# Attention operand loads issued from POOL, and a one-column product moved from POOL to ACT, in a two-block transformer kernel

## The chip, the cores and the metric

The kernel runs on one core of a Trainium2 chip. The metric is device time in microseconds of one execution, median of several runs; lower is better. The engines named below are PE (matrix products), PEld (its weight loads), DVE, ACT and POOL (elementwise work) and SP, which in the kernel before does nothing but issue DMAs. Each engine runs its own list of instructions in order.

## The reference

Two transformer blocks follow one another on a sequence of 2048 rows of width 1024, in float32. The first block is a short convolution mixer and then a stick-breaking attention with 8 heads of 64; the second has a pooled mixer and an attention over the best keys that a small index network picks. Cut to the two attentions:

```python
def _stick_breaking_attention(q, k, v):          # first block
    for blk in range(n_blocks):                   # blocks of 128 queries
        z = einsum("bhqd,bhkd->bhqk", qb, kf[:, :, :kl]) * scale
        mask = arange(kl)[None, :] < q_pos[:, None]
        log_one_minus = where(mask, log_sigmoid(-z), 0.0)
        rev = cumsum(log_one_minus, axis=3, reverse=True)
        weights = exp(where(mask, z + rev, -inf))
        outs.append(einsum("bhqk,bhkd->bhqd", weights, vf[:, :, :kl]))

def dsa_attention(q, k, v, q_idx, k_idx, w_idx):  # second block, per block of 128 queries
    logits = einsum('bqhd,bsd->bqhs', qib, kf_idx) * IDX_DIM ** -0.5
    score = einsum('bqhs,bqh->bqs', relu(logits), wb) * N_IDX_HEADS ** -0.5
    _, sel = top_k(where(causal, score, -inf), 256)
    s = einsum('bqhgd,bqkhd->bqhgk', qg, k_sel) * HEAD_DIM ** -0.5
    o = einsum('bqhgk,bqkhd->bqhgd', softmax(where(valid, s, -inf)), v_sel)
```

## The kernel before

A float32 product is made of three PE passes over a rounded part and a rest of each operand (L119 to L121, `lin<-act,fixedr`). The program is a set of Python generators, one for each phase, which `build()` runs one after the other or merges two by two: `merge((a, wa), (b, wb))` takes steps from both in the proportion of their weights. Behind that, a scheduler fixes for every engine one static order of its instructions, before anything runs; an engine that reaches an instruction whose data or buffer isn't there waits, and everything behind it on that engine waits too.

The phases in order: a (convolution mixer), b (projections of the first attention), c (stick-breaking attention), d (its output projection and norms), e and e2 (projections of the second block), f (index scores, search, attention over chosen keys) and g (output projection). Halves of 1024 rows are overlapped: c(0) with b(1), c(1) with d(0), e(0), e2; f's first part with d(1), e(1), e2; and the rest of f with g.

All DMAs go through `dma()` (L75 to L77) and so stand in one order on SP: weights from DRAM (`fixed<-in_w_in_dram`), the split weights that are kept for the second half (`kept_w_in<-fixedr`) and read again (`fixedr<-kept_w_in`, `fixedr<-kept_w_out`), results on their way to DRAM (`qis<-xe`, `cata<-ff`), and the operands of both attentions.

- **Stick-breaking, phase_c.** For each pair of heads p and each chunk g of 512 queries (a group: 4 x 2 in each half, 16 in all) it loads `cq` (`crr<-qst`, two tiles of two DMAs, a ring of 3), `ck` (`crr<-kst`, a ring of 4) and `cv` (`crf<-vst`, a ring of 2). Then, for four blocks of queries, chunks of keys and the two heads a: z on PE (L535, L536), a sigmoid on ACT (L538), its complement on ACT (L545) or, on the diagonal, DVE (L543), a running product on DVE (L548), the weights as a product of shifted columns (L549), the last column by itself on POOL (L551), four transposes on PE (L555), a copy on ACT (L557), and the product with v on PE (L563). Column `left`, by which L551 scales, comes from the chunk of keys before.
- **Scores, f_score.** For each of 8 index heads a tile `fqi` (`ffr<-qis`, two DMAs, a ring of 2), products on PE (L871, L872), relu on ACT (L874), and a weighted sum on DVE (L881), begun on POOL (L876) and masked on POOL (L890).
- **Attention over chosen keys, f_block.** For each block of 128 queries and each p a tile `fq` (`ffr<-q2s`, two DMAs, a ring of 2), products on PE (L1147, L1148), a masked maximum on DVE (L1149), exp on ACT (L1161), transposes (L1170), copies (L1172), and v's product (L1178). At the end of a block POOL spreads the reciprocal of the sums (L1190), PE broadcasts it (L1194), DVE scales the result (L1196), and POOL copies one column as a marker (L1199).

POOL also adds sums of squares in the norms (L309), does small steps of rope and of the pool mixer (L719, L724, L757, L805, L808), and the last additions of phase g (L1269, L1270).

Of the kernel before, what the change touches and what calls it, by code (L numbers as in the profile page):

```python
# [19 lines left out]
P = 128  # L20
# [35 lines left out]
def merge(*gens):  # L56
    run(merged(*gens))
# [11 lines left out]
class Build:  # L69
# [4 lines left out]

    def dma(self, out, in_):  # L75
        f = lambda ap: ap.bitcast(F32) if ap.dtype == F32R else ap
        self.nc.sync.dma_start(f(out), f(in_))  # L77

# [401 lines left out]
    def load_dup(self, tag, bufs, src, a, sl):  # L480

        t = self.turn(tag, bufs)
        for d in range(2):
            self.dma(t[d * 64 : (d + 1) * 64], src[a * 64 : (a + 1) * 64, :, sl])
        return t

    def load_stack(self, tag, bufs, src, sl):

        t = self.turn(tag, bufs)
        for s in range(2):  # L490
            self.dma(t[s * 64 : (s + 1) * 64], src[:, s, sl].rearrange("(a p) n -> p a n", a=2))
        return t
# [13 lines left out]
    def phase_c(self, h):  # L506
# [3 lines left out]
        for p in range(4):  # L510
            for g in (2 * h, 2 * h + 1):
# [5 lines left out]
                for c in range(g, -1, -1):  # L517
                    cs = slice((c % 2) * CH, (c % 2 + 1) * CH)
                    kt[c] = self.load_stack("ck", 4, self.kst[p][c // 2], cs)
                    if c == g or c % 2:  # L520
                        n = HT // P if c % 2 else HT // P // 2
                        v = self.turn("cv", 2)
                        self.dma(v[:, :n], self.vst[p][c // 2][: n * P, :].rearrange("(b p) d -> p b d", p=P))
                    vt[c] = v[:, c % 2 * 4 : c % 2 * 4 + 4]
                o = self.psum("o")
                for i in range(4):
                    qs = slice(i * P, (i + 1) * P)
                    prev = [None, None]
                    for c in range(g, -1, -1):
# [3 lines left out]
                        for a in range(2):  # L533
# [16 lines left out]
                            if c < g:  # L550
                                nc.gpsimd.tensor_tensor(s[:, W - 1 : W], s[:, W - 1 : W], left, ALU.mult)  # L551
                            prev[a] = e
# [298 lines left out]
    def f_score(self, qbs):  # L851
# [6 lines left out]
        for hd in range(8):  # L858
            q = self.turn("fqi", 2)
            rows = self.qis[h][:, hd, :, gl : gl + n * P]  # L860
            for d in range(2):
                self.dma(q[d * 64 : (d + 1) * 64], rows)
            for k, qb in enumerate(qbs):
# [258 lines left out]
    def f_block(self, qb):  # L1122
# [9 lines left out]
        for p in range(4):  # L1132
            kv = p // 2
            q = self.turn("fq", 2)
            for d in range(2):
                self.dma(q[d * 64 : (d + 1) * 64], self.q2s[h][:, 2 * p : 2 * p + 2, :, qs])
            pe = []
# [140 lines left out]
    def build(self):  # L1278
# [9 lines left out]
        with (  # L1288
# [18 lines left out]
            de = self.chain(self.phase_d(0, xb), lambda: self.phase_e(0), lambda: self.phase_e2([0, 1], self.h2))  # L1307
            merge((self.ahead(self.phase_c(1), 2000), 260), (de, 300))
            self.f_setup(0)
# [134 lines left out]
```

## Time and profile before

| | us |
|---|---|
| median of 3 runs (3470.65 to 3471.43) | 3471.29 |
| the profiled execution | 3474.31 |
| its span (first to last instruction) | 3472.6 |
| PE busy | 3222.2 (93%) |
| DVE busy | 2256.2 (65%) |
| ACT busy | 1482.4 (43%) |
| POOL busy | 484.3 (14%) |

The mean granted clock of PE over the span was 0.962 of full speed. In a profile, a line such as L551 is one of the program above; out<-in are the program's tiles, with crf and crr the rings of the stick-breaking attention, ff and ffr those of phase f, and fixed, fixedr work buffers. A wait is put down to whatever ended last before the waiting instruction. Issuing a DMA isn't counted as busy; SPq is SP's queue of DMAs.

### The profile page before, as it was taken

Reading aid. Unit: us, or ns where it says so; the run is one execution under the profiler, and the core shown is the slowest. Engines: PE = TensorE matmul, PEld = TensorE weight load, DVE = VectorE, ACT = ScalarE, POOL = GpSimd, SP = SyncE. Lnnn points to the kernel's source line nnn. Section 1 sums busy time; section 2 is a strip of 40 time slices with the busy share of each in tenths; the row PEclk is TensorE's granted clock in tenths of the full one; section 3 lists DMA queues with packets and bytes.
Section 4 is the critical chain, followed back from the end, with each engine's and each line's share of the span. In section 5 each row is a group of like instructions: output and inputs, shape, how many; then the busy total and the mean of one; then the engine's idle time right before and its main releaser. Section 6 shows DMA issues by size and latency. Waiting matters only on the chain. (4 is left out here: it accounts for less than half of the span.)

```text
span 3472.6 us, 49120 instructions
## 1 busy us (share of the span) xinstructions
PE 3222.2 (93%) x17922; PEld 2569.6 (74%) x17922; DVE 2256.2 (65%) x4508; ACT 1482.4 (43%) x2668; POOL 484.3 (14%) x600
## 2 busy tenths in 40 slices
PE   8999999999999999988989998899898898889897
PEld 7888888888787777766767776677676676667675
DVE  5343544553535887788777787897447569888641
ACT  4111421111323444555545555563364365865561
POOL 0000110000100000142021112420200422102002
PEclk9999999999999999989999999899899999989999
DMA  3111442343464545645445444644433542115005
GB/s 108 49 47 52 157 160 83 127 131 107 143 173 140 173 130 153 200 152 139 145 152 178 131 133 137 191 149 145 153 104 107 164 158 95 47 43 174 25 29 174
DMA packets 369231, 438.66 MB, mean 126 GB/s; under 512 B 23504, under 2 KB 269776, under 8 KB 368976
## 3 DMA queue, kind: packets, MB, share of 16 engines
q1 hardware_dynamic: 368976, 435.38, 40.1%
q8 instruction: 145, 2.38, 0.3%
q14 instruction: 110, 0.90, 0.1%
HBM read 308.94 MB, written 124.78 MB: 125 GB/s over the span
## 5 line engine op out<-in xcount | busy, mean ns | idle before, releaser
L119 PE MATMUL lin<-act,fixedr 128*128 128x512 f32 x1488 | 603.6, 406 | 23.5 <-DMA fixedr<-kept_w_in 12.1
L120 PE MATMUL lin<-act,fixedr 128*128 128x512 f32 x1488 | 601.3, 404 | 12.8 <-DVE act L620 10.8
L121 PE MATMUL lin<-act,fixedr 128*128 128x512 f32 x1488 | 598.1, 402 | 0.0
L104 ACT ACTIVATE fixedr<-fixed 128x512 fp32r<-128x512 f32 x295 | 186.9, 634 | 730.0 <-PE lin L120 249.3
L548 DVE TENSOR_TENSOR_SCAN crf<-crf 128x512 f32<-128x512 f32 (+3 forms) x320 | 355.5, 1117 | 64.0 <-ACT crf L545 60.9
L119 PEld LDWEIGHTS lin<-act,fixedr 128*128 128x128 f32 x1488 | 286.8, 193 | 92.2 <-DMA fixedr<-kept_w_in 10.1
L120 PEld LDWEIGHTS lin<-act,fixedr 128*128 128x128 f32 x1488 | 286.0, 192 | 80.5 <-DVE act L620 14.9
L105 DVE TENSOR_TENSOR fixedr<-fixed,fixedr 128x512 fp32r<-128x512 f32 x295 | 204.3, 693 | 204.3 <-ACT fixedr L104 192.7
L121 PEld LDWEIGHTS lin<-act,fixedr 128*128 128x128 f32 x1488 | 285.8, 192 | 63.2
L1149 DVE CUSTOM_DVE_ANT_0 fe<-z,masks 128x512 f32<-128x512 f32 (+3 forms) x320 | 186.8, 606 | 151.7 <-PE z L1148 107.2
L557 ACT COPY crf<-tp 128x512 f32<-128x512 f32 (+3 forms) x320 | 164.5, 532 | 184.0 <-PE tp L555 166.9
L119 PE MATMUL z<-act,fixedr 128*128 128x512 f32 x584 | 231.1, 396 | 10.9 <-ACT fixedr L104 10.9
L538 ACT ACTIVATE crf<-z 128x512 f32<-128x512 f32 (+3 forms) x320 | 174.9, 548 | 136.3 <-PE tp L555 114.4
L121 PE MATMUL z<-act,fixedr 128*128 128x512 f32 x584 | 229.8, 394 | 0.0
L120 PE MATMUL z<-act,fixedr 128*128 128x512 f32 x584 | 229.7, 394 | 0.0
L1172 ACT COPY ff<-tp 128x512 f32<-128x512 f32 (+3 forms) x320 | 160.1, 522 | 156.6 <-PE tp L1170 89.4
L551 POOL TENSOR_TENSOR crf<-crf 128x1 f32<-128x1 f32 x192 | 89.0, 465 | 967.0 <-ACT crf L538 696.7
L881 DVE SCALAR_TENSOR_TENSOR sc<-ff,fixed,sc 128x512 f32<-128x512 f32 (+3 forms) x266 | 176.7, 686 | 59.4 <-ACT ff L874 58.5
L1170 PE MATMUL tp<-fixed,fe 128*128 128x128 f32 x1088 | 185.4, 292 | 30.9 <-ACT fe L1161 21.1
L874 ACT ACTIVATE ff<-z 128x512 f32<-128x512 f32 (+3 forms) x304 | 157.2, 544 | 128.9 <-PE z L872 120.8
L549 DVE TENSOR_TENSOR crf<-crf 128x511 f32<-128x511 f32 (+3 forms) x320 | 200.5, 632 | 11.2 <-DVE crf L548 0.5
L1161 ACT ACTIVATE fe<-fe,fixed 128x128 f32<-128x128 f32 (+15 forms) x128 | 165.7, 1295 | 76.6 <-DVE fixed L1160 75.8
(343 smaller groups left out, 6559.4 us busy)
## 6 DMA issues: line engine op xcount, KB each, us to landing
fixed<-in_w_in_a_dram SPq DMA_DIRECT2D x128, 256.0 KB
fixedr<-kept_w_out SPq DMA_DIRECT2D x64, 512.0 KB
kept_w_in<-fixedr SPq DMA_DIRECT2D x46, 512.0 KB
fixedr<-kept_w_in SPq DMA_DIRECT2D x46, 512.0 KB
crr<-kst SPq DMA_DIRECT2D x80, 256.0 KB
crr<-qst SPq DMA_DIRECT2D x64, 256.0 KB
fixed<-x2d SPq DMA_DIRECT2D x64, 256.0 KB
ffr<-q2s SPq DMA_DIRECT2D x128, 128.0 KB
```

What stands on the lines that cost most here:

```text
L104: nc.scalar.activation(t[:, 0], raw, AF.Copy)
L105: nc.vector.tensor_tensor(t[:, 1], raw, t[:, 0].bitcast(F32), ALU.subtract)
L119: self.nc.tensor.matmul(ps[:, :n], whi[k], a, start=k == 0, stop=False)
L120: self.nc.tensor.matmul(ps[:, :n], whi[k], b, start=False, stop=False)
L121: self.nc.tensor.matmul(ps[:, :n], wlo[k], a, start=False, stop=k == nk - 1)
L538: nc.scalar.activation(s[:, :W], z[:, :W], AF.Sigmoid)
L548: nc.vector.tensor_tensor_scan(er, er, er, left, ALU.mult, ALU.min)
L549: nc.vector.tensor_tensor(s[:, : W - 1], s[:, : W - 1], e[:, 1:W], ALU.mult)
L881: nc.vector.scalar_tensor_tensor(sc[:, c0 : c0 + m], r[:, :m], w, sc[:, c0 : c0 + m], ALU.mult, ALU.add)
L1149: nc.vector.tensor_tensor_reduce(row[:, c0 : c0 + m], z[:, :m], mb[:, c0 : c0 + m], 1.0, NEG, ALU.subtract, ALU.max, mx[:, c : c + 1])
L1161: nc.scalar.activation(row[:, :W], row[:, :W], AF.Exp, bias=nbs, scale=sc, accum_out=den[:, hd : hd + 1])
L1170: nc.tensor.transpose(tp[:, j * P : (j + 1) * P], pe[a][:, k0 : k0 + P], self.ident)
```

## The change

Three edits. The loads of cq, ck, cv, fqi and fq are issued on POOL instead of SP: 64 of `qst`, 80 of `kst`, 24 of `vst`, 112 of `qis` and 128 of `q2s`, 408 DMAs in the part of the program that runs. The product of the last column, L551 (192 times), is an ACT instruction with a per-row scale instead of a POOL product. And the weight of c(1) in its merge is 250 instead of 260.

```diff
-    def dma(self, out, in_):
+    def dma(self, out, in_, on=None):
         f = lambda ap: ap.bitcast(F32) if ap.dtype == F32R else ap
-        self.nc.sync.dma_start(f(out), f(in_))
+        (on or self.nc.sync).dma_start(f(out), f(in_))
...
-            self.dma(t[d * 64 : (d + 1) * 64], src[a * 64 : (a + 1) * 64, :, sl])
+            self.dma(t[d * 64 : (d + 1) * 64], src[a * 64 : (a + 1) * 64, :, sl], self.nc.gpsimd)
...
-            self.dma(t[s * 64 : (s + 1) * 64], src[:, s, sl].rearrange("(a p) n -> p a n", a=2))
+            self.dma(t[s * 64 : (s + 1) * 64], src[:, s, sl].rearrange("(a p) n -> p a n", a=2), self.nc.gpsimd)
...
-                        self.dma(v[:, :n], self.vst[p][c // 2][: n * P, :].rearrange("(b p) d -> p b d", p=P))
+                        self.dma(v[:, :n], self.vst[p][c // 2][: n * P, :].rearrange("(b p) d -> p b d", p=P), nc.gpsimd)
...
-                                nc.gpsimd.tensor_tensor(s[:, W - 1 : W], s[:, W - 1 : W], left, ALU.mult)
+                                nc.scalar.activation(s[:, W - 1 : W], s[:, W - 1 : W], AF.Copy, scale=left)
...
-                self.dma(q[d * 64 : (d + 1) * 64], rows)
+                self.dma(q[d * 64 : (d + 1) * 64], rows, nc.gpsimd)
...
-                self.dma(q[d * 64 : (d + 1) * 64], self.q2s[h][:, 2 * p : 2 * p + 2, :, qs])
+                self.dma(q[d * 64 : (d + 1) * 64], self.q2s[h][:, 2 * p : 2 * p + 2, :, qs], nc.gpsimd)
...
-            merge((self.ahead(self.phase_c(1), 2000), 260), (de, 300))
+            merge((self.ahead(self.phase_c(1), 2000), 250), (de, 300))
```

The scheduler makes a new order from this. PE's list is the same as before up to the start of c(0) and differs from there on.

SP of the kernel before, in c(1), where the operands of the third pair of heads are loaded (kst_1_150, qst_1_158) among the second block's weights (in_w_in) and their kept copies:

```order
L77 DMA crr<-kst_0_149 64x2x512 x2
L77 DMA qis_187<-xe 4x32x1024
L77 DMA fixed<-in_w_in_dram 128x4x128
L77 DMA kept_w_in_0_12667<-fixedr 128x1024
L77 DMA crr<-qst_1_158 64x2x512 x4
L77 DMA crr<-kst_1_150 64x2x512 x2
L77 DMA fixed<-in_w_in_dram 128x4x128
L77 DMA kept_w_in_4_12672<-fixedr 128x1024
```

POOL at the same place, as a piece of the difference (- before, + after):

```order
 L724 COPY fixed<-fixed 128x64 x4
-L551 TENSOR_TENSOR crf<-crf 128x1 x31
+L77 DMA crr<-kst_1_150 64x2x512 x2
+L77 DMA crr<-kst_0_149 64x2x512 x4
+L77 DMA crr<-qst_1_158 64x2x512 x4
+L77 DMA crr<-kst_1_150 64x2x512 x2
+L77 DMA crf<-vst_1_166 128x4x128
+L77 DMA crf<-vst_0_165 128x8x128
 L757 TENSOR_TENSOR fixed<-fixed 128x16
-L551 TENSOR_TENSOR crf<-crf 128x1
```

The loads left SP's list, where a kept weight's write stood just ahead of qst_1_158; on POOL only loads of the same group stand between L724 and them, where 31 products of L551 stood.

POOL of the kernel before in phase f, from the first scores (L876) of a pair of blocks to the end of the two blocks that are attended meanwhile:

```order
L938 TENSOR_TENSOR fixed<-fixed 128x2
L876 TENSOR_SCALAR sc<-ff,fixed 128x512
L876 TENSOR_SCALAR sc<-ff,fixed 128x384
L876 TENSOR_SCALAR sc<-ff,fixed 128x512 x4
L1190 COPY ff<-fixed 128x512
L1199 COPY fixed<-ff 128x1
L1190 COPY ff<-fixed 128x512
L1199 COPY fixed<-ff 128x1
```

The same place after, from the last two of these L876 on:

```order
L876 TENSOR_SCALAR sc<-ff,fixed 128x512
L77 DMA ffr<-qis_188 64x2x256 x2
L876 TENSOR_SCALAR sc<-ff,fixed 128x512
L77 DMA ffr<-q2s_186 64x4x128 x4
L77 DMA ffr<-qis_188 64x2x256 x2
L1190 COPY ff<-fixed 128x512
L77 DMA ffr<-q2s_186 64x4x128 x2
L1199 COPY fixed<-ff 128x1
L77 DMA ffr<-qis_188 64x2x256 x2
L77 DMA ffr<-q2s_186 64x4x128 x4
L77 DMA ffr<-qis_188 64x2x256 x2
```

Loads now stand between POOL's own steps, some behind L1190 and L1199 of a block.

ACT in c(0), where the split of the other half's rows (L81) runs between the attention's steps, as a piece of the difference:

```order
 L545 ACTIVATE crf<-z 128x512
 L81 ACTIVATE act_6796<-fixed 128x512
+L551 ACTIVATE crf<-crf 128x1
 L81 ACTIVATE act_6797<-fixed 128x512
+L551 ACTIVATE crf<-crf 128x1
 L557 COPY crf<-tp 128x256
 L538 ACTIVATE crf<-z 128x384
```

L551 stands some steps behind L538 and L545 of its chunk and ahead of later copies L557.

## Rows read from the trace of the kernel before

**Rows 1.** The page: busy time by engine, and the program's one DMA queue.

```profile
PE 3222.2 (93%) x17922; PEld 2569.6 (74%) x17922; DVE 2256.2 (65%) x4508; ACT 1482.4 (43%) x2668; POOL 484.3 (14%) x600
...
q1 hardware_dynamic: 368976, 435.38, 40.1%
```

**Rows 2.** Windows: stretch, us; busy us by engine; clock, DMA share, GB/s.

```profile
1080.00:2140.00 1060.00, 1002.70 (x6296) 789.23 (x6294) 853.80 (x1284) 546.55 (x1087) 173.77 (x258) 0.97 0.49 150
2140.00:2450.00 310.00, 265.69 (x1326) 211.77 (x1325) 251.94 (x726) 152.34 (x312) 78.35 (x77) 0.90 0.50 159
2450.00:3385.00 935.00, 828.08 (x5268) 648.50 (x5266) 647.61 (x1800) 514.76 (x858) 158.81 (x161) 0.94 0.31 99
```

**Rows 3.** Waits of PE: what it waited for, us in total, times, longest.

```profile
PE lin L119 <- DMA fixedr<-kept_w_out: 18.9, 8, 6.9
PE z L535 <- DMA crr<-qst: 16.0, 4, 13.9
...
PE z L871 <- DMA ffr<-qis: 13.7, 5, 4.6
PE lin L119 <- DMA fixedr<-kept_w_in: 12.1, 3, 5.8
...
PE o L563 <- DMA crf<-vst: 4.7, 2, 2.7
...
PE o L563 <- ACT crf L557: 2.3, 5, 0.8
```

**Rows 4.** Timeline of SP's queue, start us and length, around 1770.

```profile
1765.37 3.23 SPq L77 DMA_DIRECT2D fixed<-in_w_in_dram  x1
1768.65 3.36 SPq L77 DMA_DIRECT2D kept_w_in<-fixedr  x1
1772.10 5.47 SPq L77 DMA_DIRECT2D crr<-qst  x4
1777.62 3.57 SPq L77 DMA_DIRECT2D crr<-kst  x2
```

**Rows 5.** Timeline of PE in the same stretch; in brackets the idle time before.

```profile
1765.58 0.39 PE L536 MATMUL z<-crr 128*128 128x512 f32 x1
...
1771.04 0.39 PE L121 MATMUL lin<-act,fixedr 128*128 128x512 f32 x1
1785.30 0.45 PE L535 MATMUL z<-crr 128*128 128x128 f32 x1 [13.87 <-DMA crr<-qst]
...
1787.14 0.63 PE L119 MATMUL lin<-act,fixedr 128*128 128x512 f32 x1
```

**Rows 6.** Waits of SP's queue, the same columns.

```profile
SPq L77 <- DVE fixedr L105: 944.3, 230, 18.3
```

**Rows 7.** Waits of POOL, the same columns.

```profile
POOL crf L551 <- ACT crf L538: 696.7, 125, 190.6
...
POOL ff L1190 <- DVE fixed L1188: 312.5, 11, 55.0
...
POOL fixed L1199 <- DVE ff L1196: 154.5, 12, 23.3
```

**Rows 8.** Two moved loads by tile: ns minimum/median/maximum of one issue, first and last.

```profile
L77 SPq DMA_DIRECT2D crr<-qst x64: 512/590/1689, 1037.0 to 2048.0; - x64
...
L77 SPq DMA_DIRECT2D ffr<-qis x112: 573/597/1630, 2143.5 to 3118.8; - x112
```

**Rows 9.** L551 by line, and small ACT and POOL forms (busy us, mean ns).

```profile
L551 POOL TENSOR_TENSOR crf<-crf x192: 183/330/2244, 1116.7 to 2139.3; 128x1 f32<-128x1 f32 x192
...
L1161 ACT ACTIVATION_READ_ACCUMULATOR fe<-fe,fixed 128x1 f32 x128 | 24.2, 189 | 0.0
...
L557 ACT COPY crf<-tp 128x128 f32<-128x128 f32 x32 | 8.7, 275 | 27.0 <-PE tp L555 26.8 <-PE o L563 0.2
...
L783 ACT ACT_TABLE_LOAD x11 | 14.1, 1283 | 0.2
...
L719 POOL TENSOR_TENSOR fixed<-fixed 128x8 f32<-128x8 f32 x4 | 8.8, 2193 | 22.6 <-DVE fixed L673 18.4 <-DVE fixed L975 4.2
```

## The prediction, made before the changed kernel ran

> **What bounds the kernel now.** I read the page first: PE is busy 3222.2 us of a span of 3472.6, DVE 65%, ACT 43%, POOL 14% [rows 1]. So PE sets the end, and a change that takes no product from PE can win at most what PE idles or runs slowly, some 250 us here. Then the windows of the three stages that the change touches [rows 2]: c(0) and c(1) with their partners (1080 to 2140) leave PE idle 1060.0 - 1002.7 = 57.3 us, the first part of phase f (2140 to 2450) 44.3 us, the rest of f (2450 to 3385) 106.9 us. DVE is at 81% in the first two, so much of that idle time is a chain PE, ACT, DVE, PE. Then PE's waits [rows 3]: those for a load that the change moves are 16.0 us on qst, 13.7 us on qis and 4.7 us on vst, 34.4 us together, in 4, 5 and 2 places; kst and q2s have no row. That is the most that can be won straight from the moved loads.
>
> The largest is one gap of 13.87 us, and its cause is in SP's queue. PE last used the old tile of q at 1765.58, went idle after 1771.04 + 0.39 and went on at 1785.30 [rows 5]. In that time SP was not waiting for anything of the attention: it was at a load of the second block's weights (3.23 us from 1765.37) and at the write of a kept weight (3.36 us from 1768.65), and issued the q tiles only from 1772.10 on, 5.47 us for four, and the k tile until 1777.62 + 3.57 = 1781.19 [rows 4]. The writes of kept weights wait for the split on DVE; SP spends 944.3 us in 230 such waits (L105) [rows 6], and whatever stands behind them waits with them.
>
> **The change, part by part.** All terms are against the span of 3472.6.
>
> Moved loads, the gap at 1771: with no weight ahead of it the pair of the second q tile can be issued from 1766.0 (1765.58 + 0.39). The landing is at least 1785.30 - 1781.19 = 4.1 us after the last issue and, counted from the end of the four q issues, 7.7 us. With two issues of 0.6 us each, as on SP (590 ns, median) [rows 8], the data is there between 1766.0 + 1.2 + 4.1 = 1771.3 and 1774.9, and the gap of 13.9 us falls to 0 to 3.5 us. I take a gain of 12; its ends are 13.9 and nothing, if the landing itself was slow.
>
> Moved loads, the other ten waits: 34.4 - 13.9 = 20.5 us, 2 us each on average. Some came from SP's line and some from a buffer that PE freed late, which POOL can't mend. Ends 0 and 20.5; I take half, a gain of 10.
>
> What stays on SP: 408 issues of about 0.6 us leave it, 245 us, together with their waits for PE. PE waits 12.1 us for kept_w_in and 18.9 us for kept_w_out [rows 3], 31.0 together. Those weights are mostly late by their own buffers, so I take a fifth, a gain of 6; ends 0 and 31.
>
> The clock: after the gap matmuls take 0.63 us instead of 0.39 [rows 5], at half the granted clock; the timeline has six of that length, 6 x 0.24 = 1.4 us, and a slow start. A gain of 1.5 if the gap closes.
>
> L551 on ACT: 192 instructions of one column. The nearest ACT rows are 189 ns for a one-column read of an accumulator and 275 ns for a copy of 128 columns [rows 9], so 36 to 53 us of ACT time, in a stretch in which ACT is busy 546.6 of 1060 us [rows 2]. What hides it is that spare half; without it up to 53 us would lie on the chain to L555. PE waited for ACT's last step there (L557) only 2.3 us [rows 3]. I take a loss of 2. Nobody gains from POOL's side of it directly: the 696.7 us that L551 waited for L538 [rows 7] were empty time; it matters because loads behind L551 would have stood in it, and now they don't.
>
> Table loads: ACT's new order has two more changes of its function table, 1283 ns each [rows 9]. A loss of 1, ends 0 and 2.6.
>
> Issue on POOL: the trace has no DMA issued there. The low end is SP's 0.59 us, the high end a POOL instruction on a small tile, 2.19 us for L719 (128x8) [rows 9]. Two issues stand between a freed q buffer and the first product that needs it, at 16 group starts, so the dear end costs 16 x 2 x 1.6 = 51 us if no start has slack. Only 4 of them waited for qst before, so most have slack; I take a loss of 4, near the low end, with both ends kept. In phase f a ring of two tiles gives each load the length of a whole step p, and there the issue time hides behind PE. All 408 at 2.19 us would be 893 us, which POOL, busy 411 us of 2305 in these stages [rows 2], could hold.
>
> The trace shows that gap as time in a queue's order, not as time in moving bytes: the one queue keeps the DMA engines busy 40.1% [rows 1]. Here the Trainium skill speaks against the change ("DMA: Bandwidth & Descriptors", section "Issuing engines are not separate DMA queues"): all issuers share the same DMA engines, and issuing from several saves only the issuer's own time, usually small. By that the gap's 13.9 us would stay; the rows say that here the issuer's own time, waits of its line included, is the larger part. The same page's table of latency puts the first byte of a DMA issued by GpSimd at about 1 us, of SP's at about 0.6; no run here shows it, and by it as an estimate the term for the group starts would be at most 16 x 0.4 = 6.4 us.
>
> POOL's own line: in phase f loads stand between L876, L890, L1190 and L1199. POOL waited 312.5 us in 11 places for L1190's data and 154.5 in 12 for L1199's [rows 7]; what stands behind them in the new order, some q2s and qis pairs, waits with them, and behind the loads, which wait for PE to free a tile, stand L876 and L1190 in turn, and behind those DVE's L881 and PE's L1194. In the old order these POOL waits held nobody. Ends 0 and, with one late load of about 5 us in each of 16 blocks, 80 us. I take a loss of 4, since the scheduler puts the next block's first q2s pair ahead of L1190.
>
> The weight 250 and the new order of everything behind 1080 us have no price in the trace; 10 us either way, taken at nothing.
>
> Sum: -12 - 10 - 6 - 1.5 + 2 + 1 + 4 + 4 = -18.5, a span of 3454.1. The profiled execution took 3474.31, 1.7 us more than its span and 3.0 more than the median; so the forecast of the median is 3454.1 + 1.7 - 3.0 = 3453 us, 0.5% faster.
>
> **The rivals.** *POOL's line becomes the wait* (slower). Place: phase f from 2140 to 3385, where L1190 and L1199 end a block. Price: one qis or q2s pair per block that is issued only when the block's result is there and lands 4.1 to 7.7 us later, taken as 6 us in 8 of 16 blocks, 48 us; with the 12 us of the first gap won, 3472.6 - 12 + 48 - 1.3, some 3507 us. It decides as soon as PE's next product stands less than one landing behind L1190 in its list. For it: POOL's waits of up to 55.0 us at L1190 [rows 7] and PE's idle 106.9 us there. Against it: fq and fqi have a spare tile each, and PE's list holds other blocks' work between.
>
> *Nothing moves.* The loads are late because buffers come free late or because the bytes take their time, which is the result that the rule above would give, and the terms of ACT and POOL's line eat the rest: 3471 us, within 7.
>
> *More than the direct waits.* SP, relieved of 408 issues and their waits, delivers weights and stores in time, and the 31.0 us go too, with half the clock stretches after PE's gaps: -13.9 - 20.5 - 31.0 + 11 is about -54, 3417 us.
>
> **How the numbers follow.** A measurement of this kernel can tell about 0.2%, 7 us, from no change. Forecast (3435 to 3464): 0.45. More than that: 0.13. Nothing: 0.16. Slower by POOL's line or by ACT's: 0.26. Faster is 0.45 + 0.13 = 0.58. The range must leave out no more than 2 in 10: below 3418 I leave 0.08, above 3505 0.12, the upper end lying at the slower rival's own time.
>
> **What would show it.** In the changed profile a second DMA queue carries the moved bytes. No PE wait on crr<-qst should be longer than about 4 us (the first term), those on qis and vst together below about 10 us, those on kept_w_in and kept_w_out a little smaller. POOL's waits should name PE's z products ahead of its loads, and L1190 and L1199 as before. Wrong would be: PE waits on ffr<-q2s, which had no row before, or on POOL's L1190 (the slower rival); waits of L555 or L563 on ACT well over 10 us (L551's price); a new wait on crr<-qst at many group starts (a dear issue).

## The result, and the profile after

The changed kernel took 3493.91 us, median of 4 runs (3491.7 to 3496.96), beside 3470.97 for the kernel before: a ratio of 1.0068 with a 95% interval of 1.005 to 1.0085, so 0.7% slower. The forecast of 3453 us had the wrong sign; that the time lies inside the range is owed to the slower rival, at whose time the range ended.

The profiled execution has a span of 3495.1 us, 22.5 more than before, at a mean granted clock of 0.96 (0.962 before). The page, busy us by engine and then the two DMA queues (packets, MB, share):

```profile
PE 3232.0 (92%) x17922; PEld 2568.1 (73%) x17922; DVE 2256.1 (65%) x4508; ACT 1517.8 (43%) x2862; POOL 644.4 (18%) x816
...
q1 hardware_dynamic: 276432, 355.66, 31.1%
q0 software_dynamic: 25984, 79.72, 8.4%
```

PE's 17922 matmuls took 9.8 us longer than in [rows 1], so 12.7 of the 22.5 us are new idle time and 9.8 are longer matmuls, at the lower granted clock. The second queue carries 79.72 MB of the moved loads, in 25984 packets; the first queue has 92544 fewer. On POOL the 408 issues are counted as busy, some 254 us by their medians, and lift POOL from 484.3 to 644.4 although L551 has left it.

The windows of [rows 2] again (stretch, us; PE, PEld, DVE, ACT, POOL busy; clock, DMA share, GB/s):

```profile
1080.00:2140.00 1060.00, 1008.70 (x6356) 789.13 (x6354) 855.53 (x1287) 583.04 (x1283) 181.47 (x229) 0.98 0.49 151
2140.00:2450.00 310.00, 249.30 (x1185) 196.82 (x1186) 232.73 (x665) 141.07 (x294) 118.19 (x151) 0.87 0.45 146
2450.00:3385.00 935.00, 827.37 (x5191) 646.25 (x5189) 657.28 (x1827) 513.60 (x857) 261.88 (x316) 0.94 0.31 103
```

Up to 2140 PE did 60 matmuls more than before in the same time: the stick-breaking attention gained. From 2140 to 2450 it did 1185 where it had done 1326, with a clock of 0.87 for 0.90. The loss starts there, at the start of phase f.

PE's waits, for [rows 3] (waited for; us, times, longest):

```profile
PE tp L1170 <- ACT fe L1161: 39.3, 23, 7.0
PE lin L119 <- ACT pp L81: 29.0, 1, 29.0
PE lin L119 <- DMA fixedr<-kept_w_out: 14.0, 4, 6.7
...
PE z L871 <- DMA keys<-kis: 10.6, 1, 10.6
...
PE lin L119 <- DMA fixedr<-kept_w_in: 5.8, 2, 5.3
...
PE z L871 <- DMA ffr<-qis: 2.1, 1, 2.1
...
PE z L1147 <- DMA ffr<-q2s: 1.1, 1, 1.1
...
PE z L535 <- DMA crr<-qst: 0.9, 2, 0.7
```

Three of these rows as they were before:

```profile
PE lin L119 <- ACT pp L81: 27.5, 1, 27.5
PE tp L1170 <- ACT fe L1161: 21.1, 12, 5.3
...
PE z L871 <- DMA keys<-kis: 11.4, 1, 11.4
```

The moved loads did come in time: qst, qis, vst (0.2) and q2s together cost PE 4.3 us, where qst, qis and vst had cost 34.4. What grew is the wait for ACT, added up over all rows 153 us for 94 before, and in it the wait for exp (L1170 on L1161), 39.3 us for 21.1. The 29.0 us at L119 were 27.5 before; they come back below.

The moved loads by tile, for [rows 8] (ns of one issue, minimum/median/maximum), and L551 in its new place, for [rows 9]:

```profile
L77 POOL DMA_DIRECT2D crr<-qst x64: 587/598/698, 1038.2 to 2024.6; - x64
...
L77 POOL DMA_DIRECT2D ffr<-qis x112: 587/597/676, 2137.5 to 3134.6; - x112
...
L551 ACT ACTIVATE crf<-crf x192: 278/324/450, 1118.8 to 2132.9; 128x1 f32<-128x1 f32 x192
```

POOL's waits, for [rows 7], of which L551's has gone:

```profile
POOL crr L77 <- PE z L536: 479.5, 35, 65.4
...
POOL ffr L77 <- PE z L1148: 288.8, 41, 16.5
...
POOL fixed L1199 <- DVE ff L1196: 96.1, 9, 27.1
...
POOL ff L1190 <- DVE fixed L1188: 75.8, 11, 28.9
```

POOL's loads wait for PE to free a tile, and L1190 and L1199 wait less than before (312.5 and 154.5 us).

**How the stages are cut below.** Positions in us shift from kernel to kernel, so stages are cut at the same piece of work in each trace. Stage c goes from the first L535 to the last L563. Stage f1 goes from there until PE has reached both the 2505th L119 instruction (of 2928 in every kernel) and the one wait of L871 for `keys<-kis`, the second half's keys. Stage f2 goes from there to the last L1178. The two marks of f1 come in either order: in before, e5, e6, e10 and e18 the wait (7.5 to 12.1 us) stands ahead of that L119, in the others behind it. A cut at the L119 alone, which the expectations use (356 us for before, 377 for after, 375 for e1, 347 for e4, 382 for e3), counts the wait in some kernels and not in others.

Before these stages take 1059, 355 and 896 us, after 1046, 388 and 893. So c gained 12, f1 lost 33, and f2 gained 3. Each stage is read off one execution. Six kernels have the same PE order up to the end of c as the kernel before, and their c is 1050 to 1059 us; four have e4's, with 1036 to 1046. A difference of less than 10 us in a stage is therefore not told apart from run to run.

### The profile page after: what moved, and what is told of

Same layout as the page of the kernel before. It is cut to its first block, busy times and chain, and to the rows that moved or that the text cites. A ratio compares the mean times of both kernels' runs of the same rounds, so it can differ in the third digit from the quotient of the medians.

```text
span 3495.1 us, 48760 instructions
## 1 busy us (share of the span) xinstructions
PE 3232.0 (92%) x17922; PEld 2568.1 (73%) x17922; DVE 2256.1 (65%) x4508; ACT 1517.8 (43%) x2862; POOL 644.4 (18%) x816
## 3 DMA queue, kind: packets, MB, share of 16 engines
q0 software_dynamic: 25984, 79.72, 8.4%
## 5 line engine op out<-in xcount | busy, mean ns | idle before, releaser
L119 PE MATMUL lin<-act,fixedr 128*128 128x512 f32 x1488 | 604.1, 407 | 37.7 <-ACT act L81 13.7
L119 PEld LDWEIGHTS lin<-act,fixedr 128*128 128x128 f32 x1488 | 286.0, 192 | 108.3 <-ACT act L81 15.3
L119 PE MATMUL z<-act,fixedr 128*128 128x512 f32 x584 | 231.1, 396 | 11.3 <-ACT fixedr L104 11.3
L881 DVE SCALAR_TENSOR_TENSOR sc<-ff,fixed,sc 128x512 f32<-128x512 f32 (+3 forms) x266 | 194.4, 753 | 67.7 <-ACT ff L874 67.2
L557 ACT COPY crf<-tp 128x512 f32<-128x512 f32 (+3 forms) x320 | 164.6, 532 | 150.8 <-PE tp L555 138.2
L1170 PE MATMUL tp<-fixed,fe 128*128 128x128 f32 x1088 | 184.8, 288 | 46.1 <-ACT fe L1161 39.3
L538 ACT ACTIVATE crf<-z 128x512 f32<-128x512 f32 (+3 forms) x320 | 175.3, 548 | 104.8 <-PE tp L555 97.0
L309 POOL TENSOR_TENSOR acc<-acc,sq 128x1024 f32<-128x1024 f32 x42 | 105.8, 2527 | 560.3 <-ACT sq L307 560.3
L1161 ACT ACTIVATE fe<-fe,fixed 128x128 f32<-128x128 f32 (+15 forms) x128 | 165.8, 1296 | 81.2 <-DVE fixed L1160 80.6
```

Source lines behind the costliest of these rows:

```text
L119: self.nc.tensor.matmul(ps[:, :n], whi[k], a, start=k == 0, stop=False)
L538: nc.scalar.activation(s[:, :W], z[:, :W], AF.Sigmoid)
L881: nc.vector.scalar_tensor_tensor(sc[:, c0 : c0 + m], r[:, :m], w, sc[:, c0 : c0 + m], ALU.mult, ALU.add)
L1161: nc.scalar.activation(row[:, :W], row[:, :W], AF.Exp, bias=nbs, scale=sc, accum_out=den[:, hd : hd + 1])
L1170: nc.tensor.transpose(tp[:, j * P : (j + 1) * P], pe[a][:, k0 : k0 + P], self.ident)
```

## The experiments

Theories. **A, POOL's line:** loads in POOL's order hold up POOL's own work or each other (the prediction's slower rival). **B, the issuer:** the DMA path of POOL itself is slower, or disturbs DVE. **C, the order:** the scheduler's static order of all engines changes with the edit, and that is what costs. The expectations, written as the work went on, use other letters: in them A (later A2, A3) is POOL's line, B (later B2, B3) is the order, and C is a price of L551 on ACT. In all kernels below the matmuls are the same; the kernel before took between 3470.97 and 3473.29 us beside them, so medians can be set side by side.

| kernel | F loads on | C loads on | L551 on | weight | us | ratio to before, interval | c | f1 | f2 |
|---|---|---|---|---|---|---|---|---|---|
| before | SP | SP | POOL | 260 | 3471 | | 1059 | 355 | 896 |
| after | POOL | POOL | ACT | 250 | 3493.9 | 1.0068 (1.0050 to 1.0085) | 1046 | 388 | 893 |
| e1_f_loads | POOL | SP | POOL | 260 | 3497.9 | 1.0069 (1.0052 to 1.0085) | 1055 | 387 | 889 |
| e2_f_loads_l551 | POOL | SP | ACT | 260 | 3484.9 | 1.0033 (1.0022 to 1.0043) | 1036 | 387 | 892 |
| e3_all_loads | POOL | POOL | POOL | 260 | 3499.7 | 1.0073 (1.0057 to 1.0090) | 1051 | 392 | 890 |
| e4_l551 | SP | SP | ACT | 260 | 3455.7 | 0.9954 (0.9937 to 0.9971) | 1039 | 356 | 890 |
| e5_qis_only | POOL (qis) | SP | POOL | 260 | 3475.5 | 1.0012 (1.0001 to 1.0022) | 1053 | 372 | 880 |
| e6_q2s_only | POOL (q2s) | SP | POOL | 260 | 3496.0 | 1.0066 (1.0049 to 1.0083) | 1050 | 377 | 897 |
| e7_f_loads_on_act | ACT | SP | ACT | 260 | 3472.7 | 0.9995 (0.9984 to 1.0007) | 1046 | 374 | 895 |
| e8_c_loads_l551_270 | SP | POOL | ACT | 270 | 3454.3 | 0.9945 (0.9929 to 0.9962) | 1045 | 353 | 884 |
| e9_before_270 | SP | SP | POOL | 270 | 3441.2 | 0.9920 (0.9895 to 0.9945) | 1034 | 356 | 885 |
| e10_before_255 | SP | SP | POOL | 255 | 3481.7 | 1.0028 (1.0018 to 1.0038) | 1062 | 356 | 892 |
| e11_l551_270 | SP | SP | ACT | 270 | 3435.2 | 0.9900 (0.9874 to 0.9926) | 1042 | 367 | 857 |
| e12_l551_250 | SP | SP | ACT | 250 | 3448.0 | 0.9934 (0.9915 to 0.9953) | 1050 | 348 | 881 |
| e13_after_4tiles | POOL | POOL | ACT | 250 | 3487.4 | 1.0029 (1.0016 to 1.0042) | 1051 | 376 | 894 |
| e14_all_loads_4tiles | POOL | POOL | POOL | 260 | 3485.7 | 1.0036 (1.0022 to 1.0049) | 1051 | 378 | 886 |
| e18_l551_one_tile | SP | SP | ACT | 260 | 3458.3 | 0.9950 (0.9934 to 0.9967) | 1039 | 367 | 892 |
| e17_before_4tiles_260 | SP | SP | POOL | 260 | 3467.9 | 0.9987 (0.9976 to 0.9999) | 1053 | 346 | 896 |
| e19_pool_touch | SP | SP | POOL | 260 | 3468.8 | 0.9984 (0.9970 to 0.9998) | 1056 | 350 | 891 |
| e16_before_4tiles_270 | SP | SP | POOL | 270 | 3456.2 | 0.9959 (0.9944 to 0.9974) | 1029 | 361 | 897 |

F loads are those of qis and q2s, C loads those of qst, kst and vst. No run has the whole change with the weight 260 or 270.

### Which part of the change costs

**e1_f_loads**, the loads of phase f alone:

```diff
+                self.dma(q[d * 64 : (d + 1) * 64], rows, nc.gpsimd)
...
+                self.dma(q[d * 64 : (d + 1) * 64], self.q2s[h][:, 2 * p : 2 * p + 2, :, qs], nc.gpsimd)
```

> Part alone: only the q2s and qis loads of phase f go to POOL, the weight stays 260. The changed kernel lost some 31 us between the end of c(1) and the first use of the second half's keys (2133 to 2528 there, 2139 to 2503 before). Theory A (POOL's line): loads on POOL in phase f hold up POOL's own steps and each other, so this kernel is slow too: 3471 + 25 to 35, about 3500, with the loss in that stretch. Theory B (new order): the loads arrive in time and the loss came from the static order that the scheduler happened to make; then this kernel, with another order, lies anywhere within 3471 plus or minus 25, and PE's waits on ffr loads stay below 10 us whatever the time.

3497.86 us, 26 more than before. The F loads alone lose as much as the whole change, and they lose it in f1 (387 us for 355). The time is the one that POOL's line was given; PE's waits on these loads stay small (5.8 us on qis, none on q2s), as the order was given.

**e2_f_loads_l551**, e1 with L551 on ACT:

```diff
+                                nc.scalar.activation(s[:, W - 1 : W], s[:, W - 1 : W], AF.Copy, scale=left)
```

> The loads of phase f on POOL and L551 on ACT, weight 260; the loads of phase c stay on SP. Theory A: as with the phase f loads alone, about 3500. Theory B: another order, anywhere within 3471 plus or minus 25, not the sum of the two parts' own differences. If L551 on ACT has a price of its own (C), it is the difference from the phase f loads alone and from 1080 to 2140: 2 to 53 us.

3484.86 us, 13 less than e1, so not the 3500 of POOL's line. L551 on ACT is a gain, in c (1036 us for 1055); f1 keeps its 387.

**e3_all_loads**, all 408 loads on POOL, L551 left there, weight 260:

```diff
+            self.dma(t[d * 64 : (d + 1) * 64], src[a * 64 : (a + 1) * 64, :, sl], self.nc.gpsimd)
...
+                        self.dma(v[:, :n], self.vst[p][c // 2][: n * P, :].rearrange("(b p) d -> p b d", p=P), nc.gpsimd)
...
+                self.dma(q[d * 64 : (d + 1) * 64], rows, nc.gpsimd)
...
+                self.dma(q[d * 64 : (d + 1) * 64], self.q2s[h][:, 2 * p : 2 * p + 2, :, qs], nc.gpsimd)
```

> All moved loads on POOL, L551 stays on POOL too, weight 260. Theory A: about 3500 or more, since phase c's loads now stand behind L551 too; PE waits on crr<-qst at many group starts. Theory B: within 3471 plus or minus 25, PE's waits on moved loads below 10 us in phase f; in phase c they show what L551 in the same line costs, between 0 and some 15 us.

3499.72 us, within 2 of e1: the C loads add nothing that can be told, even behind L551 in POOL's line, and PE's waits on qst at many group starts did not come (3.6 us in 2 places).

**e4_l551**, L551 alone (the line of e2, all loads on SP):

```diff
-                                nc.gpsimd.tensor_tensor(s[:, W - 1 : W], s[:, W - 1 : W], left, ALU.mult)
+                                nc.scalar.activation(s[:, W - 1 : W], s[:, W - 1 : W], AF.Copy, scale=left)
```

> Part alone: L551 on ACT, no load moved, weight 260. Theory A: no loss in phase f, 3471 plus 0 to 5 from ACT. Theory B: its order is new too, so it can lie as far from 3471 as the others, up to 25 us either way, though nothing of phase f was touched. Theory C (ACT pays): slower by 10 to 50 us with the loss between 1080 and 2140.

3455.65 us, 16 less than before, though no load moved; only the order's range has it. PE's waits in e4:

```profile
PE z L535 <- DMA crr<-qst: 1.2, 2, 1.0
```

The gap of 13.87 us of [rows 5] is gone with the q tiles still in SP's line, so another order of that line can close it too.

### Which load, and is it POOL

**e5_qis_only** and **e6_q2s_only**, one half of e1 each:

```diff
+                self.dma(q[d * 64 : (d + 1) * 64], rows, nc.gpsimd)
```

> Only the 112 qis loads of the scores go to POOL, weight 260. With all phase f loads on POOL PE's order put 15 first passes of lin between the first and the seventh score product (before: none) and 55 up to the nineteenth (before: 19), so that d(1)'s products were used up early and PE idled in the norm behind them. Theory B2 (the order follows from who issues qis): the same order, 3490 to 3500. Theory A2 (POOL's line on the chip, q2s behind L1190 and L1199): most of the loss is gone, 3470 to 3480, whatever the order.

```diff
+                self.dma(q[d * 64 : (d + 1) * 64], self.q2s[h][:, 2 * p : 2 * p + 2, :, qs], nc.gpsimd)
```

> Only the 128 q2s loads go to POOL, weight 260. Theory B2: the first scores stand as before, 3471 within 10. Theory A2 (q2s behind L1190 and L1199): 3490 to 3500, with PE waits on ffr<-q2s or on POOL.

e5 3475.49, e6 3495.98 us. Both totals lie in the ranges given to POOL's line, and neither in that of the order; but the waits that POOL's line should have shown in e6 did not come: PE has no wait on q2s, and waits 7.0 us for POOL in all. By the total the blame falls on q2s (+23) and hardly on qis (+3). By the stage it falls on each: f1 is 372 and 377 us, where it is 355 with neither and 387 with both. e5 gets it back in f2, 880 for 896, and no row was found that tells why. The totals add up (3 and 23 alone, 26 together), so this pair does not speak against a cost that comes with each load.

**e7_f_loads_on_act**, e2 with the F loads in ACT's queue:

```diff
+                self.dma(q[d * 64 : (d + 1) * 64], rows, nc.scalar)
...
+                self.dma(q[d * 64 : (d + 1) * 64], self.q2s[h][:, 2 * p : 2 * p + 2, :, qs], nc.scalar)
```

> L551 on ACT, and the phase f loads are issued on ACT instead of POOL; the loads of phase c on SP, weight 260; its neighbour with the loads on POOL took 3484.9 and with them on SP 3455.7. Nothing of phase f is in POOL's line. Theory A2: the loss in phase f goes, 3456 plus what 240 issues of 0.6 us cost ACT (0 to 40 us, and ACT's waits for a free tile). Theory B2: what counts is where the first scores stand in PE's order; if they are spread over lin as with POOL, about 3485; if not, A2 and B2 agree.

3472.71 us, between e4 (3455.65) and e2 (3484.86), and f1 is 374 us, between 356 and 387. Taking the loads from SP already costs without POOL in it; POOL is worse. The time lies in the wide range given to POOL's line, but a loss without POOL speaks against A and B as the whole cause. That the loads in ACT's line have a price of their own is not excluded, though PE's waits for ACT in f1 are 10.2 us, about as in e4 (9.2).

### What the order does by itself

**e8_c_loads_l551_270** (C loads on POOL, L551 on ACT), **e9_before_270**, **e10_before_255**, **e11_l551_270** and **e12_l551_250** set the weight; e9 and e10 change nothing else:

```diff
-            merge((self.ahead(self.phase_c(1), 2000), 260), (de, 300))
+            merge((self.ahead(self.phase_c(1), 2000), 270), (de, 300))
```

> The loads of phase c on POOL and L551 on ACT, phase f's loads on SP, weight 270. Both theories: no loss in phase f, so faster than before: 3450 to 3460, as with L551 alone (3455.7), less up to 10 if the loads' own queue gains; PE's waits on crr<-qst below 4 us.

> The kernel before with weight 270 alone: how far a new order by itself moves the time. If orders scatter by 10 us or more, L551's gain of 16 us at 260 may be an order and no property of the edit; if this stays within 5 of 3471, the gain belongs to the edit.

> The kernel before with weight 255 alone, as the last: within 5 of 3471, or a scatter of 10 us or more.

> L551 on ACT, no load moved, weight 270; against the kernel before at 270. If the gain belongs to the edit (a product that no longer waits in POOL's line, or a shorter one on ACT): 16 us below the kernel before at the same weight. If it was the order at 260: anywhere within 20 us of it.

> L551 on ACT, no load moved, weight 250, which is the weight of the changed kernel: it tells what of the changed kernel's 3493.9 is due to its moved loads at the same weight. If the loads of phase f cost 26 to 29 us here too, this is 3465 to 3468; if the gain of L551 holds at any weight, 3456.

The kernel before takes 3481.7 at 255, 3471.3 at 260 and 3441.2 at 270: 40 us between them with the same instructions on the same engines, but for two loads of ACT's function table that the kernel with 270 has fewer. This is more than the whole change moved. And the change comes apart: e12 is the change without the moved loads, 3448.0 us, a gain of 23 and better than either of its two expectations; the moved loads, with the order that they bring, then cost 3493.9 - 3448.0 = 46 us. e8 came out as expected; e11 is 6 us below e9 and not 16, so the gain of L551 is not one figure either.

e8 against e11 shows how an order makes such a cost. The C loads end with c, and c differs by 3 us; f1 is 14 us shorter in e8, f2 27 longer, with not one load of these two stages moved in either. PE's wait at L119 for ACT's L81 in e8:

```profile
PE lin L119 <- ACT pp L81: 26.8, 1, 26.8
```

The same row of e11:

```profile
PE lin L119 <- ACT pp L81: 0.4, 1, 0.4
```

This is one idle stretch of PE (at 2665 to 2692 in e8), where a product of the second half waits for its input; 19 of the 20 kernels have it, with 26 to 29 us, the kernels before and after too. e11's order alone has none, and with 3435.2 us it is the fastest, 1.0% below before. The 19 us that the C loads seem to cost at weight 270 are this gap, less what f1 gains, in stages that have none of these loads.

### Why f1 is longer with the F loads on POOL

The cleanest pair is after against e12: the same weight, the same L551, and the same instructions but for the issuer of the loads and four more loads of ACT's function table in after. Windows from the end of c to the 2505th L119, the columns as above. Of the kernel before, where the wait for `keys<-kis` and some 20 matmuls more stand ahead of that L119:

```profile
2151.00:2506.00 355.00, 302.98 (x1485) 243.03 (x1486) 279.03 (x780) 164.84 (x330) 85.12 (x76) 0.90 0.51 162
```

Of the kernel after:

```profile
2140.00:2516.00 376.00, 309.49 (x1464) 245.97 (x1465) 278.75 (x779) 164.40 (x328) 137.14 (x166) 0.88 0.45 147
```

Of e12:

```profile
2143.00:2481.00 338.00, 297.18 (x1463) 237.32 (x1463) 275.11 (x780) 164.87 (x327) 85.48 (x74) 0.93 0.51 161
```

Of e19, which is told below:

```profile
2151.00:2492.00 341.00, 300.64 (x1463) 240.40 (x1463) 273.47 (x779) 164.45 (x327) 98.81 (x114) 0.92 0.51 160
```

After and e12 do the same work there (1464 and 1463 matmuls, DVE and ACT busy alike), in 376 and 338 us. Of the 38 us, 12.3 are PE busy at a lower clock and 25.7 PE idle. A good part is lost in one place, 60 to 100 us behind the end of c, where PE does 104 matmuls in after and 172 in e12. Of after:

```profile
2200.00:2240.00 40.00, 23.89 (x104) 18.14 (x103) 34.30 (x147) 17.59 (x48) 22.95 (x22) 0.61 0.27 97
```

Of e12:

```profile
2203.00:2243.00 40.00, 32.97 (x172) 27.31 (x171) 37.36 (x128) 19.74 (x49) 16.53 (x9) 0.74 0.51 160
```

What PE waited for in the 376 us of after:

```profile
PE tp L1170 <- ACT fe L1161: 21.5, 12, 7.0
PE lin L119 <- ACT act L81: 7.3, 1, 7.3
PE lin L119 <- DVE xe L657: 7.1, 1, 7.1
...
PE o L1178 <- ACT ff L1172: 5.0, 7, 1.4
```

The same of e12:

```profile
PE lin L119 <- DMA fixedr<-kept_w_in: 8.4, 3, 5.1
PE z L871 <- DMA ffr<-qis: 8.0, 4, 4.0
PE tp L1170 <- ACT fe L1161: 7.5, 5, 2.9
```

After waits for ACT and DVE, and less for loads than e12: 9.0 us (5.8 on kept_w_in, 2.1 on qis, 1.1 on q2s) for 16.4. It isn't late data, then. PE reaches the transposes (L1170) and the projections (L119) before ACT and DVE are done with what they need. That this is a matter of what stands between in the lists of the three engines is inferred from the waits, not shown by a run of its own.

**e13_after_4tiles** and **e14_all_loads_4tiles**, after and e3 with two more tiles of q_idx for the first scored pair of blocks (the tiles of fq lie idle then), so that scores need not be spread out by the loads; **e17_before_4tiles_260** and **e16_before_4tiles_270** are the same on the kernel before:

```diff
-            q = self.turn("fqi", 2)
+            q = self.turn("fqj" if qbs[0] == 2 and hd % 2 else "fqi", 2)
...
+        self.rings["fqj"] = r[:, :2].rearrange("p n (s m) -> p n s m", s=2)
```

> The changed kernel with four instead of two tiles for the qis loads of the first scored pair of blocks (the idle fq tiles take every other head); all moved loads stay on POOL. In PE's order the 13th score product now stands behind 18 lin products of d(1) instead of 34, the 19th behind 43 instead of 55. Theory B3 (late first scores in the static order leave DVE idle and lengthen phase f's first part): that part falls from 377 us by about half of its 25 us excess or more, the time from 3494 to 3470 to 3483. Theory A3 (POOL's line on the chip): as many loads stand in POOL's line as before, so 377 and 3494 within 5, or slower.

> The same four tiles in the kernel with all moved loads on POOL, L551 on POOL and weight 260, which took 3499.7 and 382 us in the first part of phase f. Theory B3: 355 to 370 us there, 3475 to 3488. Theory A3: unchanged within 5.

> The control: the kernel before with four tiles for the first scored pair, loads on SP. The 13th score product stands behind no lin product instead of 3, the 19th behind 15 instead of 19. Both theories: about as before, 3462 to 3475; if it gains as much as the kernels with loads on POOL, the four tiles help for another reason.

> The kernel before at weight 270 (3441.2) with four tiles for the first scored pair, loads on SP: if the 19 us that the four tiles took off the first part of phase f at 260 hold here, 3425 to 3438; if they are given back later as at 260, 3436 to 3446.

f1 falls by 12 us (388 to 376) and 14 (392 to 378) with the loads on POOL, and by 10 (355 to 346) without, at weight 260; at 270 it rises by 5 (356 to 361), with a total 15 us longer than e9, outside both its ranges. e13 lies between its two ranges, e14 and e17 in theirs. The more tiles do about as much without POOL's loads as with them, so the late first scores are not what sets POOL's loads apart.

**e18_l551_one_tile**, the counterpart: e4 with one tile of q_idx for six of the eight heads of that pair, which spreads the first scores as in after, with the loads on SP:

```diff
+            q = self.turn("fqi", 1 if qbs[0] == 2 and hd < 6 else 2)
```

> No load on POOL: L551 on ACT, weight 260 (3455.7 and 347 us), but the qis loads of the first scored pair have one tile instead of two for six of eight heads. In PE's order the first scores are then spread over lin as with qis on POOL (13th behind 27, 19th behind 50 lin products; with two tiles 3 and 24). Theory B3: the first part of phase f takes 370 to 380 us and the kernel 3475 to 3485, without POOL. Theory A3: 347 us and 3456, plus at most 10 for the loads that are no longer fetched ahead.

3458.29 us beside 3455.65 for e4, in the range given for no cost of late scores. f1 is 11 us longer (367 for 356), f2 the same (892 for 890); as the profiled execution lies 6 us above the median for e18 and 4 below for e4, most of the 11 may be that. PE's waits to the 2505th L119 show another reason than in after:

```profile
PE z L871 <- DMA ffr<-qis: 23.1, 5, 11.7
...
PE tp L1170 <- ACT fe L1161: 6.5, 9, 1.9
```

Late scores cost waits for qis, not waits for exp.

**e19_pool_touch**, the kernel before with a copy of one column on POOL into each tile of fqi and fq, ahead of its load; the loads stay on SP, but must wait for POOL's line (120 copies are added work):

```diff
+            nc.gpsimd.tensor_copy(q[:, 0, 0:1], self.mark2)
...
+            nc.gpsimd.tensor_copy(q[:, 0, 0, 0:1], self.mark2)
```

> The kernel before (weight 260, L551 on POOL) with one more POOL instruction ahead of each tile of q2s and qis: a copy of one column into the tile, which waits as the moved loads do until PE has freed it; the loads themselves stay on SP and wait for the copy. So every phase f load hangs on POOL's line, but no DMA is issued there. If the line is the cause: the first part of phase f takes 370 to 385 us instead of 356 and the kernel 3485 to 3500, as with the loads on POOL (375 us, 3497.9). If the DMA issued on POOL, as the order reckons with it, is the cause: 350 to 362 us and within 10 of 3471.

3468.79 us, a ratio of 0.9984, and f1 350 us for 355; by the cut of the expectation 341, shorter than both of its ranges. POOL's groups by line (busy us, mean ns, idle time before them and its causes) show the copies in the place of the loads:

```profile
L860 POOL CAST ffr<-fixed 128x1 fp32r<-128x1 f32 x56 | 17.6, 316 | 199.2 <-PE z L872 153.9 <-PE z L873 37.3 <-DMA ffr<-q2s 7.9
...
L1136 POOL CAST ffr<-fixed 128x1 fp32r<-128x1 f32 x64 | 17.0, 266 | 289.6 <-PE z L1149 193.3 <-PE z L1150 83.9 <-DMA ffr<-qis 6.5
```

POOL waits 468 us for PE to free these tiles (368.5 in after, for the loads), and holds its L876, L1190 and L1199 behind them, and nothing is lost. So waits for a free tile in POOL's line are not the cause.

The copies leave out another wait that the loads have: a load of qis also waits for the store that puts qis into DRAM (`qis<-xe`). In after, POOL stands 12.6 us at such a load, behind it the mask of a score (L890), and behind that a step of the search on ACT (L971) and one on DVE (L972):

```profile
2424.81 2.40 POOL L77 DMA_DIRECT2D ffr<-qis  x4 [12.62 <-DMA qis<-xe]
2427.19 0.33 POOL L890 TENSOR_SCALAR_AFFINE_SELECT sc<-sc 128x128 f32<-128x128 f32 x1
2427.55 1.15 ACT L971 ACTIVATE masks<-sc,fixed 128x1024 int8<-128x1024 f32 x1 [10.41 <-POOL sc L890]
2428.83 0.15 DVE L972 TENSOR_SCALAR fixed<-fixed 128x1 f32<-128x1 f32 x1 [11.91 <-ACT masks L971]
```

All six kernels with both qis and q2s on POOL have this wait of ACT, 10.4 to 13.8 us; in the other 14 ACT waits at most 2.6 us for POOL in f1. In e5, with qis alone, POOL stands 21.5 us at such a load, and DVE waits 25.3 us for POOL in f1, for 2.8 before. This is theory A at one spot. PE has other work while ACT waits, and no run shows how much of it reaches the end of f1; e6, which has no load of qis on POOL, loses 22 us of f1 without it.

**What the twenty traces say together.** With F loads on POOL f1 takes 372 to 392 us (8 kernels), with them on ACT 374 (e7), with them on SP 346 to 367 (11 kernels), whatever the weight, L551 and the C loads. In f1 and f2 taken together it is 1264 to 1283 against 1224 to 1258 on SP and 1268 on ACT, with e5 (1253) on the wrong side. Of A, the waits for a free tile are out, and the wait for the store of qis is seen but has no price. Of B, the waits for loads are too small for a slow transfer. C is shown to move 40 us by itself, and the waits in f1 look like its kind. What isn't shown is the last step, that the same order with another issuer would take the time of the order: the scheduler makes an order for each issuer, and no run has one with the other's. So why every order with POOL's F loads comes out long in f1 stays open.

## Why the prediction was wrong, step by step

- **The gap at 1771** (12 us gained): closed, the longest wait for qst is 0.7 us. e12, with the same weight and L551 and the loads on SP, has it:

```profile
PE z L535 <- DMA crr<-qst: 16.0, 4, 12.8
```

So in this change the gain of 12 belongs to the loads, as predicted. It is not theirs alone: with the C loads on SP the longest such wait is 12.8 to 14.4 us in seven kernels, 6.2 and 6.5 in e11 and e10, and 1.0 to 2.3 in the other six; with them on POOL it is 0.5 to 2.7 in all five.

- **The other ten waits** (10): right in kind, larger. With the gap, waits for moved loads fell from 34.4 to 4.3 us, 30.1 for 22; against e12, which has 37.8, they fell by 33.5.
- **SP's relief** (6): kept_w_in and kept_w_out fell from 31.0 to 5.8 + 14.0 = 19.8, so 11.2, but not by the moved loads: e12 has 18.5 with the loads on SP,

```profile
PE lin L119 <- DMA fixedr<-kept_w_out: 10.1, 4, 7.1
...
PE lin L119 <- DMA fixedr<-kept_w_in: 8.4, 3, 5.1
```

and the three other kernels with all loads on POOL (e3, e13, e14) have 36 to 39. That the change came out on the side of this term is luck.

- **The clock** (1.5 gained): the wrong way. PE's matmuls took 9.8 us more over the span; in f1 alone the granted clock is 0.88 for e12's 0.93, with 12.3 us more of PE busy for the same products.
- **L551 on ACT** (2 lost): 192 x 0.324 = 62 us of ACT, above the 53 of the upper bound, and still hidden: PE's wait at L563 for L557 went from 2.3 to 4.7 us in 5 places. Run alone it is a gain of 16 us at 260 and 6 at 270. "Nobody gains from POOL's side of it" can't be kept; how much of the 16 is the order and how much L551 itself wasn't told apart.
- **Table loads** (1): two more, 1283 ns each, as said.
- **Issue on POOL** (4): 598 ns for qst and 597 for qis, as on SP [rows 8]; only the 24 loads of vst are dearer, 897 ns for 384. The dear end of 2.19 us was far off; the term is next to nothing.
- **POOL's own line** (4, and the slower rival): PE's waits for POOL rose from 5.4 to 9.9 us. The rival's price came near the time (3507 against 3494), but its mechanism, loads late behind L1190, did not happen: POOL waits less at L1190 and L1199 than before, and PE waits 1.1 us on q2s. What did happen is the hold of L890 behind a load of qis, told above, whose price is open. A rival whose number is near is not thereby shown.
- **"The weight 250 and the new order ... 10 us either way, taken at nothing"** is the step that failed. The waits on loads fell by more than the terms for them, by 41 us (30.1 + 11.2); all other idle time of PE rose by 54.0 and its matmuls by 9.8, 63.8 us that the sum had at nothing. Against e12 it is the same: PE's waits on moved loads fall by 33.5 us, its waits for ACT, DVE and POOL rise by 36, 11 and 9, and its matmuls take 26 us longer. A weight alone already moves the time from 10 us slower (255) to 30 faster (270), and the whole change without its loads gains 23, so that a sum of -18.5 with this term at nothing had no sure sign. That the term is larger than its bounds is shown; how much of the 46 us of the moved loads is their order and how much POOL's line stays open.

The rule of the Trainium skill that was weighed ("DMA: Bandwidth & Descriptors", section "Issuing engines are not separate DMA queues") says that several issuers save only the issuer's own time, usually small. Here the time in SP's line was not small, 33.5 us of PE's waits against e12, and the kernel did not gain from its going. The Trainium skill also warns ("SBUF — State Buffer", section "SBUF: two separate sides") that a DVE instruction in a mode with two ports locks GpSimd out while GpSimd has a DMA's descriptors to write, and its section "A bandwidth-pool intuition that's wrong (but worth ruling out)" gives for a DMA some 620 ns alone against 3100 ns in such an overlap. The trace does not show it here: the longest of POOL's 408 issues took 0.937 us (vst, where the median is 0.897), beside a DVE that was busy 81% of the time from 1080 to 2140, and whatever the landings took, PE waited 4.3 us for them.

## What to carry to other kernels

Where a scheduler lays out every engine anew from the edit, the direct terms of an edit can be the smaller part: run a null change of the order first (here a weight, 40 us), and take its spread as the bound of the unknown term. Before a gain or a gap is booked to an edit, compare kernels that differ in that edit alone: here that kept the gap for the moved loads and took SP's relief from them. And a long idle stretch that nearly every order has, like the 26 to 29 us at L119, is a better aim than an issuer: the one order without it was the fastest.

## What was not expected of the hardware

A DVE instruction of one or two columns can take as long as two or three POOL instructions that run beside it. The timeline of after, POOL, DVE and PE, in f1 (start us, length, in brackets the idle time before):

```profile
2206.29 4.62 POOL L309 TENSOR_TENSOR acc<-acc,sq 128x1024 f32<-128x1024 f32 x2
2206.33 4.61 DVE L1160 SCALAR_TENSOR_TENSOR fixed<-fixed 128x1 f32<-128x1 f32 x1
...
2211.18 0.16 DVE L1160 SCALAR_TENSOR_TENSOR fixed<-fixed 128x1 f32<-128x1 f32 x1
2211.61 0.47 PE L1170 MATMUL tp<-fixed,fe 128*128 128x128 f32 x1 [4.84 <-ACT fe L1161]
...
2218.12 0.93 POOL L876 TENSOR_SCALAR sc<-ff,fixed 128x256 f32<-128x256 f32 x1
2218.38 5.32 DVE L992 TENSOR_TENSOR fixed<-fixed 128x2 f32<-128x2 f32 x1
2219.01 4.66 POOL L309 TENSOR_TENSOR acc<-acc,sq 128x1024 f32<-128x1024 f32 x2
```

L1160 takes 0.16 us a moment later; begun just after POOL's two sums of squares it took 4.61, to their end. L992, begun within L876, took 5.32, to the end of L876 and the two sums behind it, where it took 0.15 five us earlier. exp (L1161) waits for L1160, and PE's next transpose (L1170) stood 4.84 us idle. The Trainium skill has this ("SBUF — State Buffer", section "SBUF: two separate sides": a DVE instruction with two inputs in SBUF and a GpSimd one that reads SBUF take one pair of ports in turn, the later blocking wholly), and the trace agrees; here DVE was held through two and three POOL instructions in a row. Its sum does not tell the kernels apart: what DVE's instructions took above their median while L309 ran adds up in f1 to 26.0 us in after and 23.6 in e12. Where it falls differs; in after these two fall in the 40 us in which PE does 104 matmuls for e12's 172, and no run tells what that costs.
